# SwiGLU experts of one core: gate and up side by side in each column tile, values turned in 32x32 squares on VectorE, and another order of experts

## The chip, the core and the metric

The kernel runs on one core of one Trainium2 chip. The metric is device time in microseconds (us) of one execution; lower is better. TensorE multiplies matrices, VectorE (DVE), ScalarE (ACT) and GpSimd (POOL) do the elementwise work, and SyncE (SP) issues the DMA transfers.

## The reference

A two-layer block over 256 latent tokens and 256 context tokens of width 1024. Most of the text below is about the last part, the expert layer:

```python
def swiglu(h, w_gate, w_up, w_down):
    return (jax.nn.silu(h @ w_gate) * (h @ w_up)) @ w_down

def moe_swiglu(h, router_w, router_b, w_gate, w_up, w_down):
    ...
    out = jnp.zeros_like(h)
    for e in range(N_EXPERTS):          # 8 experts, each 1024 x 3584, top 2 of 8 per token
        out = out + combine[..., e:e + 1].astype(h.dtype) * swiglu(h, w_gate[e], w_up[e], w_down[e])
    return out
```

All of it is float32. Ahead of it stand adaLN modulation, RMSNorm, the Fourier, Hyena and S5 mixers of both layers and a dense SwiGLU; behind it a final RMSNorm. The change leaves what stands ahead as it is, instruction for instruction.

## The kernel before

Tokens are routed to slots. Expert 0 comes first and has 96 slots. The other seven are ranked by how many tokens they got; the four fullest get 96 slots, the other three 64 (`TURN` gives each place in the order its rank, `None` for expert 0). 96 slots are three **groups** of 32 columns, 64 slots are one group of 64; the text calls them three-group and two-group experts after their 32-column count. In the order before they come as 3 2 3 2 3 2 3 3.

The slots' tokens are TensorE's stationary operand, 32 (or 64) columns at a time, and the weights stream past them. Four 32-column matmuls of 256 columns (or two 64-column ones of 512) lie side by side in the array, `block` issues them. The gate and up weights come in **tiles** of 1 MB (128 partitions x 2 rows of k x 1024 columns) by `mload`, the down weights too: 42 tiles for an expert, 336 in all, one DMA each on SyncE's queue. They land in a ring of 17 buffers (`NRAW` = 15 and two more, `wraw`); a load into a buffer waits until TensorE has read the tile that was in it 17 loads ago.

An expert has four **column tiles** (`c`): three of 1024 hidden columns, each with four gate tiles, four up tiles and four down tiles, and a last one of 512, with four mixed and two down tiles. `gate_up` accumulates gate in the bank `pg`, up in `pu` and both of a third group in `p3`; then ScalarE and VectorE (for the third group ScalarE and GpSimd) make the SwiGLU values `sg`. `turn` transposes these on TensorE against `ident` into the bank `phT`, six 128x128 matmuls or four, and ScalarE and VectorE copy them out to `hT`. `down` accumulates in `py` and `py3`. The down tiles of a column tile are multiplied one step late: gate and up of the next column tile come first, and `turn` is slipped in behind the first of its tiles.

When an expert's last down tile is done, `leave` scales the sums (`mys`) and splits them into `myH` and `myL`; `scatter` multiplies them back to token order (`psc`) and adds them to `xtok`. `gather` collects the slots of the next two experts (`pxe`, `pcs`), in the even places of the order; `unslot` builds the scatter's matrix (`pP`). After the last expert `final` normalizes, and writes four pieces `ob`, each with its own output DMA.

All engines work through their queues in the order that a scheduler gave them when the program was built; the loads stand on SyncE's queue in the order of use.

Of the kernel before, what the change touches and what calls it, by code (L numbers as in the profile page):

```python
# [42 lines left out]
def _consts():  # L43
# [20 lines left out]
    iq = np.concatenate([p % 32 + 32 * np.arange(3)[None], p % 64], 1).astype(f32)  # L64
# [17 lines left out]
def _prep(i):  # L82
# [40 lines left out]
    m = np.empty((NE, 42, 128, 2048), np.float32)  # L123
    wg, wu, wd = (i[n][0] for n in ('moe_w_gate', 'moe_w_up', 'moe_w_down'))

    def tiles(v):
        return v.reshape(NE, -1, 2, 128, D).transpose(0, 1, 3, 2, 4).reshape(NE, -1, 128, 2048)
    for c in range(3):
        f = slice(D * c, D * c + D)
        for j, v in enumerate((wg[:, :, f], wu[:, :, f], wd[:, f])):  # L130
            m[:, 12 * c + 4 * j:12 * c + 4 * j + 4] = tiles(v)
    m[:, 36:40] = tiles(np.concatenate([wg[:, :, 3 * D:], wu[:, :, 3 * D:]], 2))
    m[:, 40:42] = tiles(wd[:, 3 * D:])
# [5 lines left out]
def build(tc, A, out, dbg=None, upto='all'):  # L139
# [1309 lines left out]
    def slots(*es):  # L1449
        Pm = mx_.tile([128, 2, 192], F32, name="Pm")  # L1450
        i = 0
        for e in es:
            n = NS[e]
# [98 lines left out]
    NC = 4  # L1552
    me = ExitStack()
    with mp_es, tc.tile_pool(name="mps", bufs=1, space=PSUM) as mps:
        def ptr(shape=(128, 512), name="ptr", dt=F32):
            return mps.tile(list(shape), dt, name=name, tag="tr", bufs=3)
# [5 lines left out]
        def mload(e, j):  # L1562
# [3 lines left out]
            if TURN[e] is None:  # L1566
                src = A['mwp'][0, j]
            else:
                if not regs:
                    regs.extend(nc.values_load(eidi[0:1, q:q + 1], engines=(mybir.EngineType.SP,), min_val=1,  # L1570
                                               max_val=NE - 1) for q in range(NE - 1))
                src = A['mwp'][bass.ds(regs[TURN[e]], 1), j].rearrange("o p n -> (o p) n")
# [4 lines left out]
        def gather(es, Pm):  # L1577
            n = sum(NS[e] for e in es)
            xe = [mp.tile([128, KD, 96], F32, name="xe", bufs=3) for e in es]
            for k0 in range(0, KD, 2):  # L1580
# [5 lines left out]
                for i in range(2):  # L1586
# [3 lines left out]
                    for x, e in zip(xe, es):  # L1590
                        o, p = x[:, k, 0:NS[e]], pb[:, i, c:c + NS[e]]
                        c += NS[e]
# [5 lines left out]
            for x, e in zip(xe, es):  # L1598
                r, w = TURN[e], GW[e]
                ns = NS[e] // w  # L1600
                cs = mp.tile([128, 3], F32, name="cs", bufs=4)
                pc = ptr((128, 3), "pcs")
                for s in range(ns):
                    for t in range(2):
                        for q in range(128 // w):
                            mm(pc[w * q:w * q + w, s:s + 1], Pm[:, t, c + w * s:c + w * s + w],
                               comb[:, t, 0:1] if r is None else combR[:, t, r:r + 1], t == 0, t == 1)
                V.tensor_copy(cs[:, 0:ns], pc[:, 0:ns])
                c += NS[e]
# [4 lines left out]
        def unslot(e):  # L1614
# [4 lines left out]
            for s in range(NS[e] // GW[e]):  # L1619
                ts_(PT[:, s], pb, iq[:, 3:4] if GW[e] == 64 else iq[:, s:s + 1], None, op0=OP.is_equal)  # L1620
# [3 lines left out]
        def block(e, o, o3, l, w, start, stop):  # L1624
            g = GW[e]
            n = 8 * g
            for s in range(NS[e] // g):
                o_ = o3 if s == 2 else o[:, n * s:n * s + n]
                for q in range(128 // g):
                    mm(o_[g * q:g * q + g], l[:, s], w[:, n * q:n * q + n], start and s != 1, stop, skip_group_check=True)  # L1630

        def groups(x, e):
            return x.rearrange("p (s w) -> p s w", w=GW[e])

        def bank(nm):
            return mps.tile([128, 512], F32, name=nm, bufs=1)


        def gate_up(e, c, xe, between=None):
            last, big = c == NC - 1, GW[e] == 32  # L1640
            pg = bank("pg")
            pu = None if last else bank("pu")
            p3 = bank("p3") if big else None
            for i, po in enumerate((pg, pu)[0:1 if last else 2]):
                for j in range(KD // 2):
                    r = mload(e, 12 * c + 4 * i + j)
                    for k in range(2):
                        kk = 2 * j + k
                        block(e, po, p3[:, 256 * i:256 * i + 256] if big else None, groups(xe[:, kk, 0:NS[e]], e), r[:, k],
                              kk == 0, kk == KD - 1)  # L1650
                    if between and i + j == 0:
                        between()
            sg = mp.tile([128, 768], F32, name="sg", bufs=2)
            if last:
                for p, n0, n1 in ((pg, 0, 512), (p3, 512, 768))[0:2 if big else 1]:
                    act(sg[0:64, n0:n1], p[0:64, 0:n1 - n0], AF.Silu)
                    tt_(sg[0:64, n0:n1], sg[0:64, n0:n1], p[64:128, 0:n1 - n0], op=mul)
                return sg
            act(sg[:, 0:512], pg, AF.Silu)
            if big:  # L1660
                t3 = mp.tile([128, 512], F32, name="t3", bufs=1)
                act(t3, p3, AF.Copy)
                act(sg[:, 512:768], t3[:, 0:256], AF.Silu)  # L1663
                gtt(sg[:, 512:768], sg[:, 512:768], t3[:, 256:512], op=mul)  # L1664
            tt_(sg[:, 0:512], sg[:, 0:512], pu, op=mul)  # L1665
            return sg


        def turn(e, c, sg):
            nr = 64 if c == NC - 1 else 128  # L1670
            hT = mp.tile([128, 6, 128], F32, name="hT", bufs=2)
            for j0, j1 in ((0, 4), (4, 6))[0:2 if GW[e] == 32 else 1]:
                pb = ptr((128, 4, 128), "phT")
                for j in range(j0, j1):
                    PE.transpose(pb[:, j - j0, 0:nr], sg[0:nr, 128 * j:128 * j + 128], ident[0:nr, 0:nr])  # L1675
                o, p = hT[:, j0:j1, 0:nr], pb[:, 0:j1 - j0, 0:nr]
                if j0:
                    V.tensor_copy(o, p)
                else:
                    act(o, p, AF.Copy)  # L1680
            return hT

        def down(e, c, hT, py, py3):
            g = GW[e]
            ni = g // 16
            last = c == NC - 1
            hT = hT if g == 64 else hT.rearrange("p (s i) m -> p i s m", s=3)
            nf = 4 if last else 8
            for j in range(nf // 2):
                r = mload(e, 40 + j if last else 12 * c + 8 + j)  # L1690
                for f2 in range(2):
                    f = 2 * j + f2
                    q, i = divmod(f, ni)
                    l = hT[:, i:i + 1] if g == 64 else hT[:, i]
                    block(e, py, py3, l[:, :, g * q:g * q + g], r[:, f2], c == 0 and f == 0, last and f == nf - 1)
# [3 lines left out]
        def leave(e, py, py3, cs):  # L1699
            w = GW[e]  # L1700
            ys = fin.tile([128, 768], F32, name="mys")
            yH, yL = (fin.tile([128, 768], F32R, name=n_) for n_ in ("myH", "myL"))
            n = 8 * w
            m = NS[e] // w * n
            for s in range(m // n):
                stt(ys[:, n * s:n * s + n], py3 if s == 2 else py[:, n * s:n * s + n], cs[:, s:s + 1],
                    gf4 if w == 32 else gf2, op0=mul, op1=mul)
            act(yH[:, 0:m], ys[:, 0:m], AF.Copy)
            tt_(yL[:, 0:m], ys[:, 0:m], yH[:, 0:m].bitcast(F32), op=sub)
            return yH, yL  # L1710

        def scatter(e, parts, PT):
            w = GW[e]
            n, nq, ns = 8 * w, 128 // w, NS[e] // w
            if w == 32:
                pbs = [ptr(name="psc") for _ in range(3)] + [bank("py3")]
            for t in range(2):
                if w == 64:
                    pbs = [ptr(name="psc") for _ in range(2)]
                c0 = n * t if w == 32 else 0  # L1720
                for s in range(ns):
                    for i in range(2):
                        for q in range(nq):
                            mm(pbs[q][:, c0:c0 + n], PT[w * q:w * q + w, s, t * 128:t * 128 + 128],
                               parts[i][w * q:w * q + w, n * s:n * s + n], s + i == 0, s == ns - 1 and i == 1)
                if w == 64:
                    for q in range(nq):
                        x = xtok[:, t, n * q:n * q + n]
                        tt_(x, x, pbs[q], op=add)
            if w == 32:  # L1730
                for q in range(nq):
                    x = xtok[:, :, n * q:n * q + n]
# [158 lines left out]
```

## Time and profile before

| what | value |
|---|---|
| median of 3 runs | 1871.48 us (1868.33 to 1875.23) |
| profiled execution | 1871.33 us |
| its span, first to last instruction | 1869.5 us |
| TensorE busy | 1743.8 us, 93% of the span |
| VectorE, ScalarE, GpSimd busy | 797.4, 473.5, 546.7 us |
| mean granted TensorE clock | 0.964 |
| DMA over the span | 506.45 MB, mean 271 GB/s |

Busy time is an average over stages of different kinds; the profile's slices of 46.7 us show where the expert stage lies: from about 987 us to the end. A matmul in float32 leaves two records in the trace, and the ends of matmuls are modelled, so that a busy TensorE can hide short waits.

### The profile page before, as it was taken

The page shows a single profiled execution, that of the slowest core. Times are in us where ns is not written, and L with a number is a line of the kernel's source. Part 1 is how long each engine was busy: PE and PEld are TensorE (multiplying, and loading weights), DVE is VectorE, ACT ScalarE, POOL GpSimd, SP SyncE. Part 2 cuts the span into 40 slices and gives each one's busy share as a digit, 9 for nine tenths or more (in the row PEclk, how much of TensorE's full clock was granted, in tenths as well). Part 3 has the DMA queues.
Part 4 walks back from the last instruction along what each step waited for, and adds up shares of the span by engine and source line. Part 5 has one row for each costly group of instructions (what it writes and reads, how often), then busy time and mean ns, then how long its engine had stood idle before and what let it go on. Part 6 is the DMA issues. An engine that isn't in the chain of part 4 may idle for free. (4 is left out here: it accounts for less than half of the span.)

```text
span 1869.5 us, 41578 instructions
## 1 busy us (share of the span) xinstructions
PE 1743.8 (93%) x17977; PEld 1143.8 (61%) x17977; DVE 797.4 (43%) x1445; ACT 473.5 (25%) x842; POOL 546.7 (29%) x561
## 2 busy tenths in 40 slices
PE   7889898899999899988899999999999999899995
PEld 4666667877767677788786653456336643456563
DVE  7589978875686766366952011011101110001012
ACT  4333224454444443244341010001000100000001
POOL 5965435568786665022410000000000000000000
PEclk6988999999999999999998999999999999999998
DMA  8234335434545664354659989999999999999980
GB/s 294 84 117 121 121 116 196 131 128 149 182 160 182 205 202 158 128 166 136 198 228 419 405 340 422 419 419 419 420 421 419 419 419 421 420 419 420 419 361 29
DMA packets 150705, 506.45 MB, mean 271 GB/s; under 512 B 18478, under 2 KB 78704, under 8 KB 106480
## 3 DMA queue, kind: packets, MB, share of 16 engines
q1 hardware_dynamic: 150512, 503.70, 70.7%
q8 instruction: 143, 2.34, 0.5%
q14 instruction: 50, 0.41, 0.1%
HBM read 489.34 MB, written 14.32 MB: 269 GB/s over the span
## 5 line engine op out<-in xcount | busy, mean ns | idle before, releaser
L151 PE MATMUL pg<-raw,xe 128*32 128x256 f32 (+1 forms) x2944 | 264.4, 409 | 5.6 <-DMA raw<-in_mwp_dram 5.6
L151 PE MATMUL py<-raw,hT 128*32 128x256 f32 (+1 forms) x3696 | 263.1, 399 | 4.9 <-DMA raw<-in_mwp_dram 3.2
L1664 POOL TENSOR_TENSOR sg<-sg,t 128x256 f32<-128x256 f32 x15 | 11.0, 733 | 841.4 <-ACT sg L1663 841.4
L443 POOL TENSOR_TENSOR pd<-ar,crow 128x1024 f32<-128x1024 f32 x88 | 224.0, 2546 | 108.7 <-ACT pd L444 85.7
L195 DVE TENSOR_TENSOR wl<-raw,wh 128x1024 fp32r<-128x1024 f32 x109 | 188.1, 1730 | 93.6 <-ACT wh L194 91.9
L151 PEld LDWEIGHTS py<-raw,hT 128*32 128x32 f32 (+1 forms) x3696 | 130.5, 112 | 125.1 <-issue 43.5
L1665 DVE TENSOR_TENSOR sg<-sg,pu 128x512 f32<-128x512 f32 x24 | 16.5, 688 | 429.6 <-PE pu L151 429.6
L151 PE MATMUL pu<-raw,xe 128*32 128x256 f32 (+1 forms) x2208 | 192.8, 407 | 0.7 <-DMA raw<-in_mwp_dram 0.7
L151 PE MATMUL p<-raw,xe 128*32 128x256 f32 x2240 | 185.9, 379 | 0.0
L151 PEld LDWEIGHTS pg<-raw,xe 128*32 128x32 f32 (+1 forms) x2944 | 110.2, 113 | 112.5 <-issue 54.3
L194 ACT ACTIVATE wh<-raw 128x1024 fp32r<-128x1024 f32 x109 | 114.5, 1054 | 167.6 <-PE pacc L151 83.5
L151 PE MATMUL pgu<-fhL,wh 128*128 128x512 f32 (+1 forms) x376 | 146.6, 390 | 5.0 <-DVE fhL L546 5.0
L151 PE MATMUL pgu<-fhH,wl 128*128 128x512 f32 (+1 forms) x360 | 143.6, 400 | 5.6 <-DVE wl L195 5.6
L151 PE MATMUL pgu<-fhH,wh 128*128 128x512 f32 (+1 forms) x392 | 147.4, 387 | 1.4 <-ACT sg L1275 0.8
L151 PEld LDWEIGHTS pu<-raw,xe 128*32 128x32 f32 (+1 forms) x2208 | 85.8, 113 | 79.8 <-issue 35.9
L444 ACT ACTIVATE pd<-pd 128x1024 f32<-128x1024 f32 x88 | 93.1, 1058 | 134.5 <-POOL pd L443 131.4
L151 PEld LDWEIGHTS p<-raw,xe 128*32 128x32 f32 x2240 | 80.2, 110 | 46.8 <-issue 0.5
L151 PE MATMUL pacc<-hL,wh 128*128 128x256 f32 (+1 forms) x248 | 89.3, 361 | 5.2 <-POOL hL L505 4.6
L151 PE MATMUL pacc<-hH,wh 128*128 128x256 f32 (+1 forms) x248 | 87.8, 364 | 4.4 <-DVE hq L834 2.5
L151 PE MATMUL pacc<-hH,wl 128*128 128x256 f32 (+1 forms) x248 | 87.7, 355 | 1.7 <-DVE wl L195 1.7
L151 PE MATMUL pacc<-HH,wh 128*128 128x512 f32 (+1 forms) x192 | 76.2, 398 | 12.7 <-DVE xT L1219 11.5
L151 PEld LDWEIGHTS pgu<-fhL,wh 128*128 128x128 f32 x376 | 72.5, 193 | 23.2 <-DVE fhL L546 6.3
(611 smaller groups left out, 2780.4 us busy)
## 6 DMA issues: line engine op xcount, KB each, us to landing
raw<-in_mwp_dram SPq DMA_DIRECT2D x336, 1024.0 KB
ar<-in_adaT_dram SPq DMA_DIRECT2D x64, 512.0 KB
raw<-in_w_in_dram SPq DMA_DIRECT2D x14, 1024.0 KB
raw<-in_fwg_dram SPq DMA_DIRECT2D x11, 1024.0 KB
raw<-in_fwu_dram SPq DMA_DIRECT2D x11, 1024.0 KB
raw<-in_fwd_dram SPq DMA_DIRECT2D x11, 1024.0 KB
raw<-in_adaN_dram SPq DMA_DIRECT2D x8, 1024.0 KB
ar<-in_adaN_dram SPq DMA_DIRECT2D x16, 512.0 KB
```

What stands on the lines that cost most here:

```text
L151: return PE.matmul(o, l, r, start=start, stop=stop, **kw)
L194: act(h, r, AF.Copy)
L195: tt_(l, r, h.bitcast(F32), op=sub)
L443: gtt(pd, r, crow[:, s], op=mul)
L444: act(pd, pd, AF.Copy, accum_out=o)
L1664: gtt(sg[:, 512:768], sg[:, 512:768], t3[:, 256:512], op=mul)
L1665: tt_(sg[:, 0:512], sg[:, 0:512], pu, op=mul)
```

## The change

The weights are stored anew: an expert now has seven column tiles of 512 hidden columns, each with four tiles that hold gate and up side by side (128 columns of the one, 128 of the other, and so on) and two down tiles; still 42 tiles of 1 MB. One accumulator `pgu` of two banks takes gate and up of all groups, and `py` is of two banks as well. Every expert is worked in 32-column groups, three or two of them. The SwiGLU values are turned by one VectorE instruction in 32x32 squares, in place of `turn`, its bank `phT` and its copies; the order of the rows of the down weights makes up for what the squares leave unturned. GpSimd has no part in it any more. The order of experts becomes 3 2 3 3 2 3 3 2. The shared bank tiles (`ptr`) are four, not three. `final` puts its four pieces into two buffers `ob`, where it had four (tags `sg` and `hT`).

```diff
-TURN = [None, 4, 0, 5, 1, 6, 2, 3]
-GW = [32 if r is None or r < 4 else 64 for r in TURN]
-NS = [96 if w == 32 else 64 for w in GW]
+TURN = [None, 4, 0, 1, 5, 2, 3, 6]
+NG = [3 if r is None or r < 4 else 2 for r in TURN]
...
-    NC = 4
+    NC = FFE // 512
...
-            return mps.tile(list(shape), dt, name=name, tag="tr", bufs=3)
+            return mps.tile(list(shape), dt, name=name, tag="tr", bufs=4)
...
+        def block(e, o, l, w, start, stop):
+            for s in range(NG[e]):
+                for q in range(4):
+                    mm(o[32 * q:32 * q + 32, s], l(s), w[:, 256 * q:256 * q + 256], start and s != 1, stop,
+                       skip_group_check=True)
+
+        def two(nm):
+            return mps.tile([128, 4, 256], F32, name=nm, bufs=1)
...
+        def gate_up(e, c, xe):
+            p = two("pgu")
+            for j in range(4):
+                r = mload(e, c, j)
+                for k in range(2):
+                    kk = 2 * j + k
+                    block(e, p, lambda s: xe[:, kk, 32 * s:32 * s + 32], r[:, k], kk == 0, kk == KD - 1)
+            n = NG[e]
+            sg, hT = (mp.tile([128, 3, 128], F32, name=n_, bufs=2) for n_ in ("sg", "hT"))
+            act(sg[:, 0:n], p[:, 0:n, 0:128], AF.Silu)
+            tt_(sg[:, 0:n], sg[:, 0:n], p[:, 0:n, 128:256], op=mul)
+            V.transpose(hT[:, 0:n], sg[:, 0:n])
             return hT
...
+        def down(e, c, hT, py):
+            for f in range(4):
+                if f % 2 == 0:
+                    r = mload(e, c, 4 + f // 2)
+                block(e, py, lambda s: hT[:, s, 32 * f:32 * f + 32], r[:, f % 2], c + f == 0, c == NC - 1 and f == 3)
...
             for c in range(NC):
-
-                def between():
-                    if pend:
-                        pend[2] = turn(*pend[0:3])
-                sg = gate_up(e, c, xe, between)
+                hT = gate_up(e, c, xe)
                 if e and c == 1:
                     scatter(e - 1, parts, PT)
...
-        pend[2] = turn(*pend[0:3])
         down(*pend)
         fgb = load_fgb(mp)
-        scatter(NE - 1, leave(NE - 1, *pend[3:5], cs0), PT)
-        final(mp, fgb, lambda: mp.tile([128, 512], F32, name="fsq2", tag="sg", bufs=2),
-              lambda i: mp.tile([128, 512], F32, name="ob", tag=("sg", "hT")[i % 2], bufs=2))
+        scatter(NE - 1, leave(NE - 1, pend[3], cs0), PT)
+        final(mp, fgb, lambda: mp.tile([128, 512], F32, name="fsq2", tag="xe", bufs=3),
+              lambda i: mp.tile([128, 512], F32, name="ob", bufs=2))
```

How the instructions stand on the engines is shown at three places. The first is TensorE's queue at the start of expert 0, before; here and below a row is a line of the code, an operation, what it writes and reads, the size of its output and how many of them follow one another.

```order
L151 MATMUL pxe<-Pm,hx 128x96 x12
L151 MATMUL pg<-raw,xe 32x256 x5
L151 MATMUL pxe<-Pm,hx 128x96 x4
L151 MATMUL pcs<-comb,Pm 32x1 x24
L151 MATMUL pgf<-ident,mcol 32x128 x8
L151 MATMUL pg<-raw,xe 32x256 x3
L151 MATMUL p_9246<-raw,xe 32x256 x4
L151 MATMUL pg<-raw,xe 32x256
L151 MATMUL pgf<-ident,mcol 64x128 x8
```

The same place with the change, on to the third pair of down tiles; a column tile is now 96 matmuls of `pgu` and then 48 of `py` of the column tile before it.

```order
L146 MATMUL pxe<-Pm,hx 128x96 x16
L146 MATMUL pcs<-comb,Pm 32x1 x24
L146 MATMUL pgf<-ident,mcol 32x128 x8
L146 MATMUL pgu<-raw,xe 32x256 x96
L146 MATMUL pP<-ident,posm 128x128 x2
L146 MATMUL pxe<-Pm,hx 128x160 x12
L146 MATMUL pgu<-raw,xe 32x256 x96
L146 MATMUL py<-raw,hT 32x256 x48
L146 MATMUL pgu<-raw,xe 32x256 x96
L146 MATMUL py<-raw,hT 32x256 x48
L146 MATMUL pgu<-raw,xe 32x256 x96
L146 MATMUL py<-raw,hT 32x256 x48
```

One `pgf` block is gone, and most of the gather for experts 1 and 2 (`pP`, `pxe` of 160 columns) has moved from the end of expert 0's third column tile to the end of its first.

The second place is TensorE's queue at the end of the last expert. Before, the last two pairs of down tiles and the turn ahead of the last two tiles:

```order
L151 MATMUL py<-raw,hT 32x256 x8
L151 MATMUL py_16010<-raw,hT 32x256 x4
L1675 MATMUL phT<-ident,sg 128x64 x6
L151 MATMUL py<-raw,hT 32x256 x8
L151 MATMUL py_16010<-raw,hT 32x256 x4
```

With the change:

```order
L146 MATMUL pP<-ident,posR 128x128 x2
L146 MATMUL pgu<-raw,xe 32x256 x64
L146 MATMUL py<-raw,hT 32x256 x32
L146 MATMUL pgu<-raw,xe 32x256 x64
L146 MATMUL py<-raw,hT 32x256 x32
L146 MATMUL pgu<-raw,xe 32x256 x64
L146 MATMUL py<-raw,hT 32x256 x64
L146 MATMUL psc<-myH,PT 128x256 x4
```

The last expert now has 64 matmuls in a step of four gate and up tiles and 32 in a pair of down tiles, and no transposes between them.

The third place is VectorE's queue at the end of the program, with what each instruction waits for (DMAHW4 and DMAHW5 tell of a DMA's landing). Before:

```order
L466 SCALAR_TENSOR_TENSOR noy<-not,noy 128x2 [waits DVE_49]
L464 TENSOR_TENSOR not<-noy 128x2 [waits DVE_49]
L465 SCALAR_TENSOR_TENSOR not<-not,nov 128x2 [waits DVE_49]
L466 SCALAR_TENSOR_TENSOR noy<-not,noy 128x2 [waits DVE_49]
L1541 SCALAR_TENSOR_TENSOR ob<-xtok,noy,fgb 128x512 [waits DMAHW4_49,DVE_49,Pool_49]
L1541 SCALAR_TENSOR_TENSOR ob<-xtok,noy,fgb 128x512 x2
```

With the change:

```order
L459 TENSOR_TENSOR not<-noy 128x2 [waits DVE_49]
L460 SCALAR_TENSOR_TENSOR not<-not,nov 128x2 [waits DVE_49]
L461 SCALAR_TENSOR_TENSOR noy<-not,noy 128x2 [waits DVE_49]
L1536 SCALAR_TENSOR_TENSOR ob<-xtok,noy,fgb 128x512 [waits DMAHW4_49,DVE_49]
L1536 SCALAR_TENSOR_TENSOR ob<-xtok,noy,fgb 128x512
L1536 SCALAR_TENSOR_TENSOR ob<-xtok,noy,fgb 128x512 [waits DMAHW4_49,DVE_49]
```

The third piece has a wait for a DMA that it did not have; ScalarE's piece, the fourth, has one too (DMAHW5).

## Rows read from the trace of the kernel before

**Rows 1.** The page's slices: GB/s in 40 equal parts of the span.

```profile
GB/s 294 84 117 121 121 116 196 131 128 149 182 160 182 205 202 158 128 166 136 198 228 419 405 340 422 419 419 419 420 421 419 419 419 421 420 419 420 419 361 29
```

**Rows 2.** Windows: length, busy us of PE, PEld, DVE, ACT, POOL, PEclk, DMA share, GB/s.

```profile
1080.00:1130.00 50.00, 50.00 (x676) 27.47 (x672) 6.72 (x20) 5.13 (x13) 0.00 (x0) 1.00 0.88 349
...
1730.00:1790.00 60.00, 60.00 (x1114) 36.48 (x1114) 6.80 (x12) 5.05 (x9) 1.47 (x2) 1.00 1.01 419
```

**Rows 3.** Waits of the DMA queue, 998:1091, then 1120:1805: us, times, longest.

```profile
SPq L1573 <- PE p L151: 53.8, 23, 5.6
...
SPq L1573 <- DMA raw<-in_mwp_dram: 508.3, 258, 3.5
```

**Rows 4.** The chain of waits in order of time: start us, us, what.

```profile
987.05 5.41 PE pxe L151 x24
...
1039.99 10.36 PE py L151 x192
...
1118.88 6.87 PE pu L151 x32
```

**Rows 5.** Windows at the end of the weights, columns as in rows 2.

```profile
1823.00:1824.00 1.00, 1.00 (x19) 0.50 (x9) 0.00 (x0) 0.00 (x0) 0.00 (x0) 1.00 0.18 74
...
1825.00:1826.00 1.00, 1.00 (x28) 0.57 (x24) 0.00 (x0) 0.00 (x0) 0.00 (x0) 1.00 0.09 16
```

**Rows 6.** Timeline after the last down tile: start us, us, engine, what, [idle before].

```profile
1848.66 1.27 DVE L1706 SCALAR_TENSOR_TENSOR mys<-py,cs,gf 128x256 f32<-128x256 f32 x3 [5.04 <-PE py L151]
1849.96 0.84 ACT L1708 ACTIVATE myH<-mys 128x768 fp32r<-128x768 f32 x1 [6.38 <-DVE mys L1706]
1850.84 0.96 DVE L1709 TENSOR_TENSOR myL<-mys,myH 128x768 fp32r<-128x768 f32 x1 [0.91 <-ACT myH L1708]
```

**Rows 7.** Groups by form, 985 us on: busy, mean ns | idle before, releaser.

```profile
L151 PE MATMUL pg<-raw,xe 128*64 128x512 f32 x384 | 88.4, 598 | 3.6 <-DMA raw<-in_mwp_dram 3.6
L151 PE MATMUL py<-raw,hT 128*64 128x512 f32 x336 | 77.3, 599 | 4.5 <-DMA raw<-in_mwp_dram 3.2 <-ACT sg L1656 1.3
L151 PE MATMUL pu<-raw,xe 128*64 128x512 f32 x288 | 64.7, 595 | 0.7 <-DMA raw<-in_mwp_dram 0.7
```

**Rows 8.** Timeline of TensorE around a turn in the last expert.

```profile
1823.09 0.61 PE L151 MATMUL p<-raw,xe 128*32 128x256 f32 x8
1823.63 0.87 PE L1675 MATMUL phT<-ident,sg 128*128 128x128 f32 x6
1824.43 0.42 PE L151 MATMUL pg<-raw,xe 128*32 128x256 f32 x4
```

**Rows 9.** Groups by form, 985 us on, of other operations.

```profile
L1665 DVE TENSOR_TENSOR sg<-sg,pu 128x512 f32<-128x512 f32 x24 | 16.5, 688 | 429.6 <-PE pu L151 429.6
L1659 ACT ACTIVATE sg<-pg 128x512 f32<-128x512 f32 x24 | 14.3, 598 | 186.1 <-PE pg L151 186.1
...
L1678 DVE COPY hT<-phT 128x256 f32<-128x256 f32 x15 | 6.3, 423 | 76.0 <-PE phT L1675 76.0
...
L151 PE MATMUL pgf<-ident,mcol 128*64 128x128 f32 x16 | 1.6, 279 | 0.0
```

**Rows 10.** The page: its head, and the queue of instructions (packets, MB, share).

```profile
span 1869.5 us, 41578 instructions
...
q8 instruction: 143, 2.34, 0.5%
```

**Rows 11.** A window in a two-group expert, columns as in rows 2.

```profile
1590.00:1600.00 10.00, 7.81 (x35) 2.03 (x32) 0.69 (x1) 0.59 (x1) 0.00 (x0) 1.00 1.02 423
```

**Rows 12.** The end: timeline of the output pieces, and a window.

```profile
1860.06 0.72 ACT L1538 ACTIVATE ob<-xtok,noy 128x512 f32<-128x512 f32 x1 [2.66 <-DVE noy L466]
...
1860.84 3.13 SPq L1542 DMA_DIRECT2D out_dram<-ob  x4
1860.86 1.74 POOL L1539 TENSOR_TENSOR ob<-ob,fgb 128x512 f32<-128x512 f32 x1 [48.84 <-ACT ob L1538]
...
1865.00:1866.00 1.00, 0.00 (x0) 0.00 (x0) 0.00 (x0) 0.00 (x0) 0.00 (x0) 0.50 0.53 193
```

More of the change, by code (lines that the diff above doesn't have):

```diff
@@ L120, in _prep @@
     a['fwg'], a['fwu'], a['fwd'] = (cc(i[n][0]) for n in ('ffn_w_gate', 'ffn_w_up', 'ffn_w_down'))
[L123 to L133, printed above, removed]
+    NC = FFE // 512
+    m = np.empty((NE, NC, 6, 128, 2048), np.float32)
+    gu = np.stack([i['moe_w_gate'][0], i['moe_w_up'][0]], 2).reshape(NE, 4, 2, 128, 2, NC, 4, 128)
+    m[:, :, 0:4] = gu.transpose(0, 5, 1, 3, 2, 6, 4, 7).reshape(NE, NC, 4, 128, 2048)
+    wd = i['moe_w_down'][0].reshape(NE, NC, 4, 2, 2, 32, D)
+    m[:, :, 4:6] = wd.transpose(0, 1, 3, 2, 5, 4, 6).reshape(NE, NC, 2, 128, 2048)
     a['mwp'] = m
@@ L1547, in load_fgb @@
         return fgb
-    NC = 4
+    NC = FFE // 512
     me = ExitStack()
@@ L1577, in gather @@
         def gather(es, Pm):
-            n = sum(NS[e] for e in es)
+            n = 32 * sum(NG[e] for e in es)
             xe = [mp.tile([128, KD, 96], F32, name="xe", bufs=3) for e in es]
@@ L1632, in groups @@
[L1632 to L1666, printed above, removed]
@@ L1669, in turn @@
[L1669 to L1680, printed above, removed]
-            return hT
@@ L1683, in down @@
[L1683 to L1695, printed above, removed]
@@ L1699, in leave @@
[L1699 to L1709, printed above, removed]
+            for s in range(NG[e]):
+                ts_(PT[:, s], pb, iq[:, s:s + 1], None, op0=OP.is_equal)
@@ new lines, in down, with leave @@
+        def down(e, c, hT, py):
[3 more added lines that the diff above has]
+                block(e, py, lambda s: hT[:, s, 32 * f:32 * f + 32], r[:, f % 2], c + f == 0, c == NC - 1 and f == 3)
+        def leave(e, py, cs):
+            n = NG[e]
+            ys = fin.tile([128, 3, 256], F32, name="mys")
+            yH, yL = (fin.tile([128, 3, 256], F32R, name=n_) for n_ in ("myH", "myL"))
+            for s in range(n):
+                stt(ys[:, s], py[:, s], cs[:, s:s + 1], gf4, op0=mul, op1=mul)
+            act(yH[:, 0:n], ys[:, 0:n], AF.Copy)
+            tt_(yL[:, 0:n], ys[:, 0:n], yH[:, 0:n].bitcast(F32), op=sub)
@@ L1710, in leave @@
             return yH, yL
         def scatter(e, parts, PT):
[L1713 to L1716, printed above, removed]
+            pbs = [ptr((128, 2, 256), name="psc") for _ in range(4)]
             for t in range(2):
[L1718 to L1721, printed above, removed]
+                for s in range(NG[e]):
@@ L1722, in scatter @@
                     for i in range(2):
[L1723 to L1732, printed above, removed]
-                    tt_(x, x, pbs[q].rearrange("p (t n) -> p t n", t=2), op=add)
+                        for q in range(4):
+                            r = slice(32 * q, 32 * q + 32)
+                            mm(pbs[q][:, t], PT[r, s, t * 128:t * 128 + 128], parts[i][r, s], s + i == 0,
+                               s == NG[e] - 1 and i == 1)
@@ L1735, in build @@
+            for q in range(4):
+                x = xtok[:, :, 256 * q:256 * q + 256]
+                tt_(x, x, pbs[q], op=add)
         (xc,) = gather((0,), Pm)
@@ L1804, in rows @@
                         SP.dma_start(w_[:, kt * j:kt * j + kt], src)
-                SP.dma_start(wd, wd_src)
+                for f, src in enumerate(wd_srcs):
+                    for i in range(2):
+                        SP.dma_start(wd[64 * f + 32 * i:64 * f + 32 * i + 32], src[:, i])
                 pg = ops.tile([128, 128], F32, name="og")
```

85 lines of the change are left out of this document (33 added, 52 removed).

## The prediction

> **What bounds the kernel now.** I read the slices of the page first, to find the stage that the change touches, then windows over that stage, then who the DMA queue waits for, then the chain of waits for the price of one weight tile, and last the end of the trace.
>
> The expert stage is the right half of the page: from slice 22 on DMA moves about 420 GB/s nearly throughout [rows 1]. One tile of 1,048,576 bytes at 420 GB/s takes 2.50 us, an expert of 42 tiles 105 us. The one clear dip is at 1080 to 1130 us, 349 GB/s [rows 2]: there the DMA queue waits for TensorE to give buffers back (53.8 us behind one kind of matmul alone between 998 and 1091), while from 1120 to 1805 it waits for its own earlier transfers, 508.3 of 685 us [rows 3]. So DMA sets the pace after the first expert, and the first expert sets when that pace begins.
>
> TensorE's price of a tile: four down tiles of a three-group expert take 10.36 us, 2.59 each; four up tiles of a two-group expert 6.87 us, 1.72 each; the stage's first matmuls, the gather of expert 0, start at 987.05 [rows 4]. Bare, a three-group expert costs 108.8 us and a two-group one 72.1, against 105 for its weights. A three-group expert therefore adds to TensorE's backlog, with its scatter, gather and transposes by 10 to 18 us, and a two-group one takes some 25 away.
>
> The order decides where that backlog is at the end. Before, two three-group experts come last. The weights are all in at about 1825.3 (16 GB/s in that microsecond, 74 two earlier) [rows 5], but `mys`, the first reader of the last down tiles' sum, starts only at 1848.66 [rows 6]. So 23 us of the span are backlog that lies behind the last byte. That is the time in question.
>
> **The change, part by part.**
>
> *The order of experts.* It ends with a two-group expert. TensorE's work from 987 to 1849 is at most 862 us less the idle time ahead of two-group tiles, 3.6 + 4.5 + 0.7 us [rows 7]: 853. The change takes about 28 from it (next paragraph), so 825 at most, and 987 + 825 = 1812 is before the last byte. In the last expert TensorE needs 72 us and its side work for what DMA brings in 105, so a backlog of up to 25 us is gone by its end. The two pairs of three-group experts in a row build up some 20 us each: less than the 23 that lie at the end of the trace of before, where 419 GB/s were held from 1730 to 1790 all the same [rows 2]. I take no lost DMA time from them (0 to 8).
>
> What stays behind the last byte is then one two-group tile, 1.72 us, 1.8 with its handoff.
>
> *The turn of the SwiGLU values.* The six transposes of a turn push two neighbouring matmul blocks apart from 0.43 to 1.34 us (1823.09 to 1824.43) [rows 8]: 0.9 us of TensorE each, 32 of them (a few cheaper), 26 to 29 us. Three lie in the first expert ahead of its hand-over. The second `gf` there, 1.6 us of matmuls [rows 9], goes too. 2.7 + 1.6 = 4.3 us: so much earlier the first expert gives its buffers back, and so much earlier DMA, which is held by them there, gets its own pace. I take -4.3 for the last byte; at least -1 (if the scheduler's other place for the first gather loses some), at most -8 (if it hides all of its side work).
>
> In their place stand on VectorE 56 multiplies and 56 transposes of at most 128x384. No row shows such a transpose: between a copy of 128x256, 0.42 us, and a multiply of 128x512, 0.69 [rows 9], I take 0.55, as the size lies between. What hides it: the transposed values are wanted only after the next four gate and up tiles, 6.9 us or more; for the very last column tile after two down tiles, 3.4 us. Even at four times the price it costs nothing.
>
> The Trainium skill, "VectorE: DVE Perf Modes", section "The three transpose paths", gives 311 ns for 128x128 on VectorE in bf16, in 32x32 blocks only. An estimate from that page is 0.93 us for three of them, above the range of the rows; the sum by it is the same, because the cover is several times longer.
>
> *One accumulator of two banks for gate and up.* The next column tile can write it only when Silu and the multiply have read it: 0.60 + 0.69 us at 128x512 [rows 9], some 1.1 to 1.3 with handoffs at 128x384. Behind it wait the next 64 or 96 matmuls. The cover is the pair of down tiles that stands between, 3.4 or 5.2 us; in the first expert, which has no earlier column tile, the gather stands there. So nothing, if the order is as printed. If that cover were gone it would be 1.3 us per column tile (second rival).
>
> *More and shorter matmuls.* Three experts go from 8 to 32 matmul records a tile at the same streamed columns: the three-group tiles run at that size already, 2.59 / 6 = 0.43 us for a group of a k row, and a two-group tile has four of these, 1.72 again. But there are 3 x 42 x 24 = 3024 more, with as many weight loads, 6048 instructions. The page has 143 packets of instructions for 41578 of them, 291 each, in 0.5% of 16 engines' 1869.5 us, 1.05 us each [rows 10]: 21 packets more, 22 us over 16 DMA engines, +1.4 us on the weights (0 to +4, if one engine gets more than its share).
>
> *The tail.* Two groups in place of three: one `mys` of 0.42, a third of `myH` 0.84 and `myL` 0.96 [rows 6] and of the last scatter, about -1.4 us. Against that the output tiles `ob` now share two buffers where there were four. The last of the four output DMAs is issued at 1863.6 (1860.84 + 3.13, less its own 0.35) and data flows until about 1866 [rows 12]: 2.5 us from issue to landing. The third and fourth `ob` must now await the first and second landing, about 1863.5 and 1864.5 (the second is issued some 0.7 us after the first). Then comes ScalarE's 0.72 and GpSimd's 1.74 us [rows 12], so the last issue is near 1867.3: +3.7 us (0 if landing is seen sooner than I think, 4.5 if late). Behind this wait nothing but the end.
>
> **Sum.** Last byte 1825.3 - 4.3 + 1.4 = 1822.4; `mys` starts 1.8 later, 1824.2 instead of 1848.66: -24.5. Tail -1.4 + 3.7 = +2.3. Together -22.2 us. The profiled execution took 1871.33 us for a span of 1869.5, and the median of the three runs is 1871.48, so the two can be read as one: 1849 us.
>
> **The rivals.**
>
> *First: part of it is lost.* Pairs of three-group experts fill the 17 buffers, or the accumulator is awaited by 0.3 us or so per column tile. 56 x 0.3 = 17 us of TensorE, of which 10 are free (1812 against 1822) and 7 count, and up to 8 us of DMA: 1856 to 1864, 1859 as a value. For it: two three-group experts follow each other twice, with a gather in the first or second. Against: 419 GB/s at the same backlog before [rows 2].
>
> *Second: slower.* The accumulator's Silu and multiply are exposed at each of 56 column tiles. Then TensorE ends at 1812 + 56 p; it decides from p = 0.2, the gain is nil at (1849 - 2.3 - 1812) / 56 = 0.62 us, and the full 1.3 ends it at 1885, 36 later than `mys` starts now, with the tail's 2.3 a time of 1910. Against it: a pair of down tiles between any two uses of the accumulator.
>
> *Third: the clock.* In stretches paced by DMA the 2.4 GHz level is lost; a two-group tile then takes 3.44 us instead of 1.72, more than its 2.50 of DMA. A backlog of 20 us is gone after 20 / (2.50 - 1.72) = 25 of the last expert's 42 tiles; the other 17 run at DMA's pace: 17 x 0.94 = 16 us back, 1865. Before, at 1590 to 1600, TensorE worked on two-group tiles at DMA's pace, busy 7.81 of 10 us, and the granted clock stayed 1.00 [rows 11]; the same duty is all that the change brings. [...]
>
> *Fourth: nothing happens,* because the weights take as much longer (other order, more instructions) as the backlog shrinks: 1871. No row speaks for it.
>
> **How the numbers follow.** What a measurement of this kernel can tell from no change is about 0.5%, 9.4 us: faster means below 1862. Forecast 0.76, its own range 1840 to 1857 (terms: -8 to -1, 0 to +4, last tile 1.7 to 3.4, tail -1.4 to +3.1, up to 8 of DMA); first rival 0.12, of which a quarter beyond 1862; third 0.05; fourth 0.03; second 0.04. Faster 0.76 + 0.09 = 0.85; the same 0.03 + 0.05 + 0.03 = 0.11; slower 0.04. A range that leaves out 2 in 10 at most is 1838 to 1862.
>
> **What would show it.** Right: all weights in near 1822, TensorE's last down tile within 3 us of it, gaps for weights ahead of its matmuls in the last expert, no `phT`, SPq waiting for DMA throughout after the first expert, a gap of 2 to 3 us ahead of the third `ob`. Wrong: idle time ahead of `pgu` that ends with `sg`, a dip in GB/s after 1200 us, clock 0.50 before 1820, or weights landing later than 1827.

## The result, and the profile after

The changed kernel takes 1848.73 us (median of 4 runs, 1846.75 to 1855.0), the kernel before 1871.06 on the same chip (4 runs): 0.9884 of it, 95% interval 0.9854 to 0.9915, or 22.3 us less. The profiled execution took 1846.75 us, the lowest of the four; its span is 1844.9.

The page of the changed kernel, head, GB/s in 40 equal slices and the queue of instructions, against [rows 1, 10]:

```profile
span 1844.9 us, 47520 instructions
...
GB/s 296 88 121 119 100 140 179 142 119 137 175 175 203 188 195 192 120 155 127 248 138 419 405 391 417 419 419 419 419 418 419 419 419 419 415 417 413 415 413 155
...
q8 instruction: 166, 2.72, 0.6%
```

The expert stage starts in slice 22 as before, and the dip in the first expert is shallower (391 where 340 stood). The windows of the first expert and of the end of the weights say it more closely, against [rows 2, 5] (length, busy us of PE, PEld, DVE, ACT and POOL, PEclk, DMA share, GB/s):

```profile
1030.00:1080.00 50.00, 49.68 (x968) 30.66 (x964) 4.18 (x10) 2.81 (x7) 0.00 (x0) 1.00 0.99 387
1080.00:1130.00 50.00, 50.00 (x944) 30.46 (x940) 8.71 (x16) 2.59 (x5) 0.00 (x0) 1.00 1.01 410
...
1800.00:1805.00 5.00, 3.92 (x72) 2.10 (x66) 0.00 (x0) 0.00 (x0) 0.00 (x0) 1.00 1.01 419
1805.00:1810.00 5.00, 4.02 (x72) 1.99 (x68) 0.00 (x0) 0.00 (x0) 0.00 (x0) 1.00 0.64 264
...
1815.00:1820.00 5.00, 3.90 (x72) 2.10 (x68) 0.00 (x0) 0.00 (x0) 0.00 (x0) 1.00 0.47 190
1820.00:1821.00 1.00, 0.56 (x16) 0.08 (x11) 0.00 (x0) 0.00 (x0) 0.00 (x0) 1.00 0.04 16
1821.00:1822.00 1.00, 1.00 (x20) 0.61 (x24) 0.00 (x0) 0.00 (x0) 0.00 (x0) 1.00 0.00 0
```

At 1800 TensorE is busy 3.9 of 5 us, where before it was busy all the time until 1848: it now waits for weights. The timeline of the end, against [rows 6, 12] (start, us, engine, what, idle time before it and its releaser):

```profile
1813.60 1.93 PE L146 MATMUL py<-raw,hT 128*32 128x256 f32 x32 [0.62 <-DMA raw<-in_mwp_dram]
...
1815.99 1.93 PE L146 MATMUL py<-raw,hT 128*32 128x256 f32 x32 [0.46 <-DMA raw<-in_mwp_dram]
...
1818.56 1.93 PE L146 MATMUL py<-raw,hT 128*32 128x256 f32 x32 [0.64 <-DMA raw<-in_mwp_dram]
...
1820.93 1.93 PE L146 MATMUL py<-raw,hT 128*32 128x256 f32 x32 [0.44 <-DMA raw<-in_mwp_dram]
1822.94 0.88 DVE L1656 SCALAR_TENSOR_TENSOR mys<-py,cs,gf 128x256 f32<-128x256 f32 x2 [8.57 <-PE py L146]
...
1832.92 1.42 DVE L1536 SCALAR_TENSOR_TENSOR ob<-xtok,noy,fgb 128x512 f32<-128x512 f32 x2
1833.70 5.22 SPq L1537 DMA_DIRECT2D out_dram<-ob  x4
1835.84 0.75 DVE L1536 SCALAR_TENSOR_TENSOR ob<-xtok,noy,fgb 128x512 f32<-128x512 f32 x1 [1.51 <-DMA out_dram<-ob]
1836.50 0.72 ACT L1533 ACTIVATE ob<-xtok,noy 128x512 f32<-128x512 f32 x1 [6.18 <-DMA out_dram<-ob]
1837.30 1.26 POOL L1534 TENSOR_TENSOR ob<-ob,fgb 128x512 f32<-128x512 f32 x1 [880.48 <-ACT ob L1533]
```

The last weights land by 1821, the last down tile ends near 1822.9, and `mys` follows at once; before, 23 us lay between. The third and fourth `ob` wait for a DMA, as the order of instructions said.

The groups by form in the stage, of its matmuls and of the transposes (busy, mean ns of one, idle time before):

```profile
L146 PE MATMUL pgu<-raw,xe 128*32 128x256 f32 x9408 | 530.4, 379 | 12.3 <-DMA raw<-in_mwp_dram 11.2 <-issue 1.0
...
L146 PE MATMUL py<-raw,hT 128*32 128x256 f32 x4704 | 271.5, 379 | 7.8 <-DMA raw<-in_mwp_dram 7.8
...
L1640 DVE STREAM_TRANSPOSE hT<-sg 128x384 f32<-128x384 f32 x35 | 20.2, 578 | 1.2
...
L1640 DVE STREAM_TRANSPOSE hT<-sg 128x256 f32<-128x256 f32 x21 | 9.4, 445 | 0.7
```

What these matmuls wait for is weights, 19 us in all, and at no place `sg`, which would be the accumulator. The DMA queue's waits from 1100 to 1805 (us, times, longest), against [rows 3]:

```profile
SPq L1568 <- DMA raw<-in_mwp_dram: 518.1, 260, 2.8
SPq L1568 <- PE pgu L146: 18.6, 25, 1.2
SPq L1568 <- PE py L146: 15.7, 12, 2.9
```

The queue waits mostly for its own transfers, as before; 34.3 us of 705 are waits for TensorE, and 30.6 of these lie before 1200, at the end of the first expert.

### The profile page after: what moved, and what is told of

It reads as the page before. It is cut to its first block, busy times and chain, and to the rows that moved or that the text cites. A ratio compares the mean times of both kernels' runs of the same rounds, so it can differ in the third digit from the quotient of the medians.

```text
span 1844.9 us, 47520 instructions
## 1 busy us (share of the span) xinstructions
PE 1708.1 (93%) x20961; PEld 1195.9 (65%) x20961; DVE 824.4 (45%) x1506; ACT 445.1 (24%) x798; POOL 535.0 (29%) x546
## 5 line engine op out<-in xcount | busy, mean ns | idle before, releaser
L146 PE MATMUL pgu<-raw,xe 128*32 128x256 f32 x9408 | 530.4, 379 | 12.3 <-DMA raw<-in_mwp_dram 11.2
L146 PEld LDWEIGHTS pgu<-raw,xe 128*32 128x32 f32 x9408 | 319.5, 110 | 207.9 <-DMA raw<-in_mwp_dram 15.4
L1639 DVE TENSOR_TENSOR sg<-sg,pgu 128x384 f32<-128x384 f32 (+1 forms) x56 | 28.2, 504 | 630.2 <-ACT sg L1638 630.2
L146 PE MATMUL py<-raw,hT 128*32 128x256 f32 x4704 | 271.5, 379 | 7.8 <-DMA raw<-in_mwp_dram 7.8
L146 PEld LDWEIGHTS py<-raw,hT 128*32 128x32 f32 x4704 | 157.8, 110 | 108.5 <-DMA raw<-in_mwp_dram 7.8
L1638 ACT ACTIVATE sg<-pgu 128x384 f32<-128x384 f32 (+1 forms) x56 | 25.2, 450 | 706.2 <-PE pgu L146 706.2
L146 PEld LDWEIGHTS pgu<-fhH,wh 128*128 128x128 f32 x392 | 73.9, 193 | 16.5 <-ACT sg L1270 1.0
L146 PEld LDWEIGHTS pgu<-fhH,wl 128*128 128x128 f32 x360 | 68.7, 191 | 23.8 <-DVE wl L190 5.3
L146 PE MATMUL pacc<-HL,wh 128*128 128x512 f32 (+1 forms) x192 | 74.6, 389 | 0.0
```

What stands on the lines that cost most here:

```text
L146: return PE.matmul(o, l, r, start=start, stop=stop, **kw)
L1638: act(sg[:, 0:n], p[:, 0:n, 0:128], AF.Silu)
L1639: tt_(sg[:, 0:n], sg[:, 0:n], p[:, 0:n, 128:256], op=mul)
```

## The experiments

**One measure for all of them.** Of the profiled execution I take four positions: the stage's start (the first `pxe`, 987.05 before [rows 4], 984.38 after), the end of the last weight packet in DMA's records, the end of the last down tile, and the end of the span. The start lies behind work that the change leaves as it is, and still it moved between 982.5 and 989.9 from run to run; so the other three are taken from it. us throughout; the time is the median (number of runs), the ratio that to the kernel before on the same chip.

| kernel | time | ratio, 95% interval | start | start to last weights | from there to the last down tile's end | from there to the end |
|---|---|---|---|---|---|---|
| before | 1871.06 (4) | | 987.05 | 837.7 | 24.3 | 20.4 |
| after | 1848.73 (4) | 0.9884, 0.9854 to 0.9915 | 984.38 | 836.1 | 2.4 | 22.0 |
| old order | 1866.08 (10) | 0.9969, 0.9958 to 0.9981 | 983.10 | 835.6 | 16.2 | 24.5 |
| order only | 1852.52 (4) | 0.9897, 0.9875 to 0.992 | 984.64 | 837.5 | 8.8 | 18.7 |
| ring of 15 | 1853.72 (4) | 0.9908, 0.9882 to 0.9934 | 982.47 | 840.7 | 2.4 | 22.2 |
| four `ob` | 1848.52 (4) | 0.988, 0.9853 to 0.9907 | 987.62 | 836.9 | 2.4 | 20.4 |
| four transposes | 1852.87 (4) | 0.9911, 0.9891 to 0.9931 | 987.16 | 837.3 | 2.4 | 22.2 |
| no cover | 1871.35 (10) | 1.0003, 0.9989 to 1.0017 | 987.73 | 849.8 | 10.9 | 22.6 |
| threes first | 1882.27 (4) | 1.0055, 1.0034 to 1.0076 | 989.93 | 866.7 | 2.4 | 22.1 |
| small gather, four `ob` | 1847.90 (5) | 0.9877, 0.9858 to 0.9896 | 987.82 | 835.1 | 2.4 | 20.7 |
| after, again | 1851.27 (5) | 0.9887, 0.9866 to 0.9908 | 983.83 | 836.7 | 2.4 | 22.1 |

The theory: the gain is the backlog of matmuls behind the last weights, and the order that ends with a narrow expert takes it away. The main rival: it is the new body, whose TensorE has no turns to do.

**The new body in the old order.**

```diff
-TURN = [None, 4, 0, 1, 5, 2, 3, 6]
+TURN = [None, 4, 0, 5, 1, 6, 2, 3]
```

> The changed kernel with the order of experts of before (groups 3 2 3 2 3 2 3 3). Theory (the order decides, because the backlog of two three-group experts at the end lies behind the last byte): the last two experts need 84 x 2.59 = 218 us of TensorE and some 10 us of gather, scatter and slot matrices, for weights that land in 210, so the last down tile ends some 18 us after the last byte instead of 2, and the tail is that of three groups, +1.4: 1866 us (1862 to 1870). Rival (the turn on VectorE and the fewer TensorE instructions make the gain): 1849. Rival (both halves share it equally): 1859.

1866.08 us, 5.2 less than the 1871.25 of before on that chip. The windows at its last weights, columns as above:

```profile
1818.00:1819.00 1.00, 1.00 (x27) 0.57 (x23) 0.00 (x0) 0.00 (x0) 0.00 (x0) 1.00 0.06 25
1819.00:1820.00 1.00, 1.00 (x24) 0.64 (x20) 0.00 (x0) 0.00 (x0) 0.00 (x0) 1.00 0.00 0
...
1838.00:1841.00 3.00, 2.69 (x44) 2.40 (x44) 0.24 (x2) 0.00 (x0) 0.00 (x0) 0.55 0.00 0
```

Its timeline behind them, columns as above:

```profile
1834.99 1.27 DVE L1656 SCALAR_TENSOR_TENSOR mys<-py,cs,gf 128x256 f32<-128x256 f32 x3 [8.67 <-PE py L146]
...
1837.25 0.39 PE L146 MATMUL psc<-myH,PT 32*128 32x256 f32 x4 [2.32 <-ACT myH L1657]
1838.24 0.56 PE L146 MATMUL psc<-myL,PT 32*128 32x256 f32 x4 [0.61 <-DVE myL L1658]
```

The weights are in at 1819 and TensorE works on without a pause until 1835: 16.2 us of backlog. The body took 8.1 of 24.3. Its profiled execution, at 1861.33, was the lowest of ten; its stage began 4 us earlier than before's. Counted from the stage's start it is 6.1 us shorter than before (835.6 + 16.2 + 24.5 against 837.7 + 24.3 + 20.4), about what the medians say.

**The old body in the new order.** The same line of `TURN`, in the kernel before.

> The kernel before with nothing but the new order of experts (3 2 3 3 2 3 3 2). Theory: the last byte lands where it did, or up to 5 us later because the pairs of three-group experts with their TensorE transposes fill the ring; mys starts 2 us behind it, the tail is 1.4 shorter: 1848 to 1853, 1850 as a value. Rival (the turn makes the gain): 1871. Rival (ring full in both pairs): 1860 and more, with a dip in GB/s in the middle of the stage.

1852.52 us, 18.7 less than before. Its `mys` in the timeline:

```profile
1830.96 0.75 DVE L1706 SCALAR_TENSOR_TENSOR mys<-py,cs,gf 128x512 f32<-128x512 f32 x1 [10.41 <-PE py L151]
```

A window in which its rate falls, columns as above:

```profile
1720.00:1740.00 20.00, 20.00 (x314) 12.65 (x316) 3.31 (x10) 2.86 (x7) 0.00 (x0) 1.00 0.85 334
```

What its DMA queue waited for from 985 to 1805 (us, times, longest):

```profile
SPq L1573 <- DMA raw<-in_mwp_dram: 317.7, 172, 3.0
SPq L1573 <- PE p L151: 161.1, 75, 9.3
SPq L1573 <- PE py L151: 103.6, 59, 4.7
```

The same two rows of the kernel before, over the same window:

```profile
SPq L1573 <- PE p L151: 73.0, 37, 9.3
SPq L1573 <- PE py L151: 38.7, 30, 2.9
```

The order by itself gives most of the gain: 18.7 of 22.3 us. The rest comes with the new body. Of its parts the turns are the likely cause, by the 26 to 29 us of TensorE that the prediction counts for them; no run takes them away alone. In the old body the queue waits 264.7 us for these two kinds of matmul to give buffers back, where it waited 111.7 in the old order. From 1700 to 1760 it waits for TensorE alone, 48.4 of 60 us: there the ring is full, and the rate falls to 334 GB/s. Its last weights come no later than before's for that (837.5 and 837.7), but the last expert is too short to work the backlog off: 8.8 us of it are left. The two parts alone, 18.7 and 5.2, add up to 23.9, about the whole.

**A ring with two buffers less.**

```diff
-NRAW = 15
+NRAW = 13
```

> The changed kernel with 15 buffers in the ring instead of 17. Theory (the first expert, held by the buffers that TensorE gives back, sets when DMA's own pace begins): each buffer less is one three-group tile later, 2 x 2.59 = 5.2 us on the last byte, and 0 to 5 more if the pairs of three-group experts now reach the end of the ring: 1854 to 1859. Rival (the number of bytes at DMA's pace alone sets the end, buffers do not): 1849.

Its GB/s in slices on the page:

```profile
GB/s 296 87 116 124 104 136 186 134 125 137 172 174 198 188 197 190 120 164 132 234 170 395 380 398 419 419 419 419 419 418 419 419 419 419 414 412 419 414 414 154
```

The last weights come 840.7 us after the start, 4.6 later, where 5.2 were expected. The loss lies in the first expert: slices 22 to 24 have 395, 380 and 398 GB/s where after has 419, 405 and 391, which is 42 / 419 of a slice of 46.2 us, 4.6 us. So buffers in the first expert set when DMA's own pace begins; what lies behind the last weights stays at 2.4 us. The median, 1853.72 us, is just below the expected range, and its runs (1850.3 to 1857.27) overlap with after's: the positions show the effect, the time alone doesn't. A larger ring was not tried.

**Four output buffers again.**

```diff
-              lambda i: mp.tile([128, 512], F32, name="ob", bufs=2))
+              lambda i: mp.tile([128, 512], F32, name="ob", bufs=4))
```

> The changed kernel with four buffers for the output pieces instead of two. Theory (the third and fourth piece wait for the landing of the first and second): that wait is gone, the last output DMA is issued some 2.5 us earlier after the first, 2 to 3 us of time, at the edge of what rounds can tell; to be read from the timeline of the end. Rival (the landing is waited for at the end of the program anyway, so nothing is won): the span from the first output piece to the end stays at 12 us.

Its timeline at the end, against that of after above:

```profile
1837.00 0.72 ACT L1533 ACTIVATE ob<-xtok,noy 128x512 f32<-128x512 f32 x1 [2.60 <-DVE noy L461]
1837.00 3.08 DVE L1536 SCALAR_TENSOR_TENSOR ob<-xtok,noy,fgb 128x512 f32<-128x512 f32 x3
1837.78 3.14 SPq L1537 DMA_DIRECT2D out_dram<-ob  x4
```

The waits are gone, the four issues take 3.14 us and not 5.22, and the end comes 1.6 us sooner (20.4 behind the last down tile, 22.0 in after), less than the 2 to 3 expected. The time, 1848.52 us, can't tell this from the rounds' spread.

**The transpose four times.** Three more of the same into a spare tile, whose values nothing reads:

```diff
+            junk = mp.tile([128, 3, 128], F32, name="junk", bufs=1)
+            for _ in range(3):
+                V.transpose(junk[:, 0:n], sg[:, 0:n])
```

> The changed kernel with three more transposes of the same size into a spare tile behind each of the 56, so VectorE's turn costs four times as much. Theory (the turn is covered by the next gate and up tiles): 1849, the same within the noise, mys 2 us behind the last byte. Rival (VectorE's turn is on TensorE's path): three more of 0.45 us at each of 56 column tiles, up to 75 us, less what TensorE has free, so 1900.

The page's row of the added ones:

```profile
L1643 DVE STREAM_TRANSPOSE junk<-sg 128x384 f32<-128x384 f32 (+1 forms) x168 | 86.4, 514 | 3.8
```

86 us more of VectorE's time, and the last weights come 837.3 us after the start, where the unchanged kernel had 836.1 and 836.7 and the one with four `ob` 836.9; nothing further back has moved. The transposes lie wholly under other work. The median, 1852.87, lies 4 above after's on another chip, and after itself had 1848.73 and 1851.27 on two: no price is shown.

**The cover taken away.** The down tiles of a column tile are multiplied right behind its own gate and up tiles, not a step later, and the loads are in that order; `leave` follows the last of them:

```diff
-                if pend:
-                    down(*pend)
...
-                pend = e, c, hT, py
+                down(e, c, hT, py)
```

> The changed kernel with the down tiles of a column tile right behind its own gate and up tiles instead of one step late; the weights are loaded in that order too. The pair of down tiles then no longer stands between the last gate and up matmul and the Silu and multiply that the next column tile waits for. Theory (the accumulator costs nothing only because of that cover): about 1.0 to 1.3 us of idle TensorE per column tile, 56 to 73 us, of which TensorE has some 15 to 20 free: 1885 to 1905, the page showing idle time ahead of pgu or py that ends with sg or hT. Rival (the ring of 17 tiles and the backlog hide it): under 1855.

Its groups on the page, columns as above:

```profile
L146 PE MATMUL pgu<-raw,xe 128*32 128x256 f32 x9408 | 550.7, 380 | 37.6 <-DVE sg L1639 37.1
...
L146 PE MATMUL py<-raw,hT 128*32 128x256 f32 x4704 | 283.8, 380 | 1.4 <-DVE hT L1640 1.4
```

The whole gain is gone: 1871.35 us, though less is lost than the 1885 to 1905 expected. TensorE now waits for `sg` to leave the accumulator, 37.1 us, or 0.66 for each of 56 column tiles, and no longer for weights. Its stage is 22.8 us longer (849.8 + 10.9 + 22.6 against 836.1 + 2.4 + 22.0): 38.5 us of new waits, less the 19 of waits for weights that they displace, is 19.5 of it; 3.3 the waits don't account for. Its waits by engine show at how many places, and its timeline one of them:

```profile
PE pgu L146 <- DVE sg L1639: 37.1, 37, 1.2
...
1061.13 2.14 PE L146 MATMUL pgu<-raw,xe 128*32 128x256 f32 x35 [1.19 <-DVE sg L1639]
```

TensorE's order puts the first matmuls of the next column tile ahead of the down tiles, as here, so nothing covers the read. Where no other work stands in the gap, the wait is 1.17 to 1.19 us behind a three-group column tile and 0.93 to 0.95 behind a two-group one, near the 1.0 to 1.3 expected. But one column tile follows another at 55 places, and the wait shows at 37 of them. At the other 18 the trace has matmuls of the gather, the scatter or the slot matrix in the gap, and at most 0.14 us of wait is left.

**All three-group experts first.**

```diff
-TURN = [None, 4, 0, 1, 5, 2, 3, 6]
+TURN = [None, 0, 1, 2, 3, 4, 5, 6]
```

> The changed kernel with the order 3 3 3 3 3 2 2 2. It also ends with a two-group expert. Theory (an order is good when the backlog stays within the ring and is gone at the end): the ring is full through five three-group experts, so DMA runs at TensorE's pace until some 582 us after 987, and the other 109 tiles at its own, 270 us: last byte about 20 us later, 1869 us (1862 to 1876), with GB/s near 390 until 1550. Rival (only the last expert's width counts): 1849.

Its GB/s in slices on the page:

```profile
GB/s 297 81 131 103 123 112 202 124 132 159 169 182 163 223 192 153 115 164 148 187 256 410 382 400 391 399 395 345 401 393 402 388 357 417 419 419 419 420 420 186
```

A window in its third expert, columns as above:

```profile
1280.00:1330.00 50.00, 50.00 (x934) 34.26 (x927) 7.86 (x21) 4.27 (x11) 0.00 (x0) 1.00 0.88 348
```

What its DMA queue waited for from 1100 to 1560:

```profile
SPq L1568 <- PE pgu L146: 244.6, 113, 9.6
SPq L1568 <- PE py L146: 120.8, 56, 3.8
```

Three narrow experts at the end leave no backlog (2.4 us), and yet it is slower than before, by about half a per cent: 1882.27 us. Through five three-group experts the ring is full, the queue waits for TensorE alone (365.4 of 460 us), and DMA is held to some 390 GB/s, which the 419 of the last three don't make up. So ending narrow is half of the rule: between the narrow ones the backlog must also fit into the ring. The last weights came 30.6 us later than in after; expected were 20, and 1862 to 1876 for the time. That a full ring costs DMA was right, its size was too low; where the other 10 us come from is left open.

**A smaller first gather.** Expert 0 gathers for expert 1 alone, and experts 1, 3 and 5 for the two behind; with four `ob`.

```diff
-                    if e % 2 == 0:
-                        es_ = (e + 1, e + 2) if e + 2 < NE else (e + 1,)
+                    if e == 0 or e % 2 and e + 2 < NE:
+                        es_ = (e + 1, e + 2) if e else (1,)
```

> The changed kernel with four output buffers, and with the gathers moved: expert 0 gathers only for expert 1, and experts 1, 3 and 5 gather for the two behind them, where experts 0, 2, 4 and 6 did. Theory (what TensorE does in the first expert delays the hand-over of buffers, and with it the last byte, one for one): the first gather is some 2 us shorter, so the last byte comes 2 us earlier after the stage's start (834 us instead of 836), and the end is 1.6 us shorter as in the run with four output buffers: 1845 (1843 to 1848). Rival (the last byte is set by the slowest DMA engine, which does not pause in the first expert): last byte at 836 after the stage's start, 1847.

**The changed kernel again,** beside it on the same chip.

> The changed kernel once more, on the same chip as the run beside it, for the comparison: 1849, the stage starting anywhere from 982 to 990 us, the last byte 836 us after it.

The last weights come 1.6 us sooner (835.1 and 836.7), little more than kernels with the same loads differ by (836.1 to 837.3), and between the 834 of the theory and the 836 of its rival: the smaller gather's part is not shown. The end comes 1.4 sooner behind the last down tile (20.7 and 22.1), as four `ob` had done. The times are 1847.9 (1846.31 to 1851.47) and 1851.27 us (1846.24 to 1854.04): the ranges overlap, so a version faster than the changed kernel is not shown.

## Why the prediction was right

1849 was forecast and 1848.73 measured. Compared from the stage's start, before and after differ by 882.4 - 860.5 = 21.9 us, against a sum of 22.2; the profiled execution's remaining 2.7 are its earlier start, which no step of the prediction speaks of. The repeat on another chip gained 20.5 (1871.78 to 1851.27), so that the median hit the forecast to within 1 us is chance. By its terms:

- **The backlog** was read as 23.4 us behind the last byte, to become 1.8, so -21.6; measured 24.3 and 2.4 to the end of the last down tile, -21.9 (before, the last packet ends at 1824.75, half a us ahead of the window that was read). That it is the order was the assumption on which everything rested, and the old body in the new order showed it, for 18.7 of the 22.3 us. What the order needs beside it stands in the prediction only as a subtraction: its 1812 counts on 28 us less of TensorE's work, and without them its own figures end at 1840, behind the last byte. With the old body 8.8 us stay.
- **The last byte** was mis-sized: -4.3 + 1.4 = -2.9 forecast, -1.6 measured (-1.0 in the repeat). Its first part held in direction, counted in GB/s: in the first expert DMA lost 2.0 + 8.5 us before (50 us each at 403 GB/s, a window of before shown below, and at 349 [rows 2], against 420) and 3.9 + 1.2 after (387 and 410), 5.4 less. But in the last five full slices it moves 413 to 417 GB/s where it held 419 before, and not for want of buffers, since its queue waits less than 1 us for TensorE from 1568 to 1800; (4 + 2 + 6 + 4 + 6) / 419 of 46.1 us each is 2.4 us given back. The other 1.4 are about what kernels with the same loads differ by (836.1 to 837.3). Instruction packets rose by 23, 21 were forecast, but the +1.4 laid on them is not shown: DMA's records have 6 to 8 of them in each of these five slices and 6 to 9 in each of slices 26 to 34, which hold 418 to 419. Of the weights' packets some 130 of 11,500 take over 0.4 us from 1570 to 1798, where the median is 0.31, against 49 of 15,200 from 1200 to 1500; what holds them up stays open.
- **The tail** was forecast at +2.3 and measured at +1.6 (20.4 to 22.0). Its two terms were both too large: the waits of `ob` cost 2.5 us from the first `ob` to the end (9.4 to 11.93), not 3.7: the landings came sooner than the prediction took, so the fourth piece starts 2.80 us after the first issue (1833.70 to 1836.50) where it had 3.7, and GpSimd's piece takes 1.26 us, not the 1.74 of [rows 12]; the two groups gave back 0.9, not 1.4.
- **The turns.** Priced at 0.55 us a transpose between two other operations of VectorE; measured 578 ns for three groups and 445 for two. The Trainium skill's figure in "VectorE: DVE Perf Modes", section "The three transpose paths", led to an estimate of 0.93 us for three squares of 128 from its 311 ns for one in bf16; one float32 instruction of that size takes 0.578. What failed is the tripling: the two measured sizes differ by 133 ns for 128 columns, which would put a single square at 312 ns, close to the page's 311; this is an estimate from the two rows, and no run here has a single square. That the turn lies under other work was shown at four times the price.
- **First rival,** part lost to a full ring: not in this kernel, whose rate after the first expert stays at 413 and above. Its mechanism is real: it is what the old body pays near 1730 and what makes threes first slower than before.
- **Second rival,** the accumulator exposed: not there either, no matmul waits for `sg`. Without the cover, its formula held: it had put nil gain at 0.62 us for each column tile, and 0.66 gave a ratio of 1.0003. The full 1.3 at each of 56 was too high: it is up to 1.2, and at 18 places other work hides it.
- **Third rival,** the clock: refuted. At 1800 to 1820 TensorE works and waits by turns, 1.93 us and then 0.44 to 0.64, busy 78%, at a granted clock of 1.00. The Trainium skill, "TensorE: Matmul & The Clock Gate", section "HAM oscillation — how this bites in real kernels", has a kernel that loses the clock between pieces of some 2 us of matmuls, but its waits for DMA are of 3 to 5 us; no wait in this stretch is so long, and no window of it shows a fall.
- **Fourth rival,** nothing: refuted by the interval.

The prediction came closer than its steps: the last byte was 1.3 us too hopeful, the tail 0.7 too dark and the backlog 0.3, and they nearly cancel. That they cancel is luck; that the order takes the backlog away is what the runs show.

## What to carry to other kernels

Where one engine is a little slower than DMA on some items and faster on others, count the backlog at the end of the stream, and put an item there on which the engine gains on DMA; but let no run of slow items pile up more than the ring holds, or DMA stops for them. An accumulator that is read by other engines needs work of another kind between two uses, and the price of losing it can be as large as the whole gain. Where an engine waits for tiles, read the times between its tiles beside the GB/s. Compare positions within a stage from the stage's own start, since work ahead of it wanders by more than the smaller terms of a sum.

## What was not expected of the hardware

The stream of weights doesn't end at full rate: from 1805 it falls to 264, 215 and 190 GB/s in steps of 5 us, to 16 in the last microsecond, with no other load asked for. Windows of the kernel before, the first one from the first expert and the others from its end, columns as above:

```profile
1030.00:1080.00 50.00, 50.00 (x922) 30.05 (x916) 1.80 (x3) 3.22 (x6) 1.47 (x2) 1.00 1.01 403
...
1805.00:1810.00 5.00, 5.00 (x98) 2.97 (x92) 0.29 (x1) 0.00 (x0) 0.00 (x0) 1.00 0.96 393
1810.00:1815.00 5.00, 5.00 (x100) 3.00 (x96) 0.39 (x1) 1.01 (x2) 0.73 (x1) 1.00 0.57 234
1815.00:1820.00 5.00, 5.00 (x100) 2.94 (x92) 0.00 (x0) 0.00 (x0) 0.00 (x0) 1.00 0.52 216
```

Both have about half the rate for some 15 us at the end of the stream. In after this does not delay the weights: TensorE, which waits for each tile, starts the last four at 1813.60, 1815.99, 1818.56 and 1820.93, 2.4 to 2.6 us apart, and those at full rate start no closer, at 1801.10, 1803.67 and 1806.07. DMA's records have 16 packets of 8 KB under way at once until about 1805 and 8 from 1808 on, each taking 0.31 us as before. So half of the 16 engines have finished their parts of the last tiles early, and the last byte waits for the other half; GB/s, a sum over all, doesn't show that, and a loss counted in it need not move the last byte one for one. Why one half is ahead stays open.

In the new body in the old order TensorE's granted clock fell to 0.55 at 1838 to 1841, after it had waited 2.32 us and then 0.61 with one short run of matmuls between. The kernel before ends with a three-group expert too; its waits at the same place were shorter in sum, and its clock is 1.00 over the window of 1848 to 1857:

```profile
1850.86 0.39 PE L151 MATMUL psc<-myH,PT 32*128 32x256 f32 x3 [1.83 <-ACT myH L1708]
...
1851.85 0.39 PE L151 MATMUL psc<-myL,PT 32*128 32x256 f32 x3 [0.60 <-DVE myL L1709]
```

From the start of the second run to the end of the scatter it is 1.6 us there (to 1853.4) and 2.7 at the fallen clock (1838.24 to 1840.9), so the fall cost about 1.1 us of that run's tail.
